# Start of layer 0 in a two-layer trunk kernel: other queues for two loads, splits ahead of norms, 1/rms spread by transposes

## The chip, the cores and the metric

The kernel runs on one core of a Trainium2 chip, as one launch. The metric is the device time of that core in microseconds, as a median over runs. Engines are TensorE (PE; its weight loads are shown as PEld), VectorE (DVE), ScalarE (ACT), GpSimd (POOL) and SyncE (SP), which here only issues transfers.

## What is computed

Two layers of a gated block on 512 tokens of width 1024, all in float32. Cut to what matters:

```python
xn = rmsnorm(x, norm1_g[i])
u_pool, q, k, v, g_a, g_b = split(xn @ w_in[i])          # 1024 -> 6144
q = rotary(rmsnorm(q, q_norm_g[i])); k = rotary(rmsnorm(k, k_norm_g[i]))
lam = exp(sum(lam_q1*lam_k1)) - exp(sum(lam_q2*lam_k2)) + lam_init
a = softmax(q1 @ k1.T * scale) - lam * softmax(q2 @ k2.T * scale)   # chunk-causal
attn = rmsnorm(a @ v, subln_g[i]) * (1 - lam_init)
merged = sigmoid(g_a) * pool_mixer(u_pool) + sigmoid(g_b) * attn
x = x + merged @ w_out[i]
hn = rmsnorm(x, norm2_g[i]); gate, up = split(hn @ w_ffn_in[i])
x = x + (silu(gate) * up) @ w_ffn_out[i]
```

## The kernel before

Every float32 operand of a large product is split in two: a high part, which ScalarE writes by a rounding copy (line 195), and a low part, which VectorE writes as the difference (line 196). A product is then a triple of matmuls: high by high, high by low, low by high (lines 264 to 266, and 473 to 475 in the first block). Weights come in pieces of 512 KB (`piece`, line 209, on SyncE's queue), seven raw buffers and six split ones deep.

In layer 0 the norm of x isn't applied ahead of the products. x comes already transposed (`in_x_t`), is scaled by the gain of the norm, from a small table `scale` of 12 KB (line 410, on ScalarE's queue; read at 458, 460 and 461), and split; 1/rms of each token is put in afterwards. `first_step(i)` loads and splits two of the eight k slices of x and of the first block's weights (q and k of head 3); the first of the four steps goes in halves of 256 KB. Ahead of it TensorE runs `WARM` matmuls on zeros. For the k slices of steps 0 and 1 all four token tiles are multiplied in turn; then, in `attention`, token by token those of steps 2 and 3, with `token_stats` behind the first: it sums the squares over the partitions with a column of `ones` and writes 1/rms to `stats[:, 1, :]` by a power on GpSimd (line 438).

Behind each token's q and k come the squares on ScalarE (600), a power on GpSimd (296), the scaling on VectorE (604) and the rotation (399 to 404). The transposes of the result (`turn`, line 285) are put off: `later(delay, what)` stores a step with a due time on a clock that counts TensorE's columns, and `run_due` runs what is due ahead of each triple of a `product`. So transposes, scores, probabilities and merges lie between the products of the next block. `spread_rms` is such a step: it brings 1/rms into a row that all partitions hold (`rms_row`), as the product of an all-ones matrix with a diagonal one; line 652 multiplies by that row.

The second block is v and the gate of head 3. Its four pieces are asked for by `wblock(KD)` behind the loop over the tokens of the first block, and then SyncE loads the vectors for lambda and the residual x. For all later blocks `wblock` stands ahead of the loop. The order that the program is written in gives the priorities; which instruction an engine's queue holds next is settled ahead of the run by a scheduler that models when each is ready, and an engine then runs its queue in order. `tc.issue_after(ins)` puts the instructions written under it behind `ins` in their engine's queue.

Of the kernel before, what the change touches and what calls it, by code (L numbers as in the profile page):

```python
# [10 lines left out]
F32 = mybir.dt.float32  # L11
# [7 lines left out]
P = 128  # L19
# [15 lines left out]

RAWS, SPLITS = 7, 6

WARM = 11

ROUNDS = ((0, 8), (8, 16), (16, 22))  # L40

# [66 lines left out]
def trunk_kernel(  # L108
# [80 lines left out]
    plan = weight_plan()  # L189
    at = [0]  # L190
    transfers = []

    def split(hi, lo, src):

        ins = nc.scalar.copy(hi, src)  # L195
        nc.vector.tensor_sub(lo, src, hi.bitcast(F32))  # L196
        return ins

    def split_half(hi, lo, src):
# [4 lines left out]
    def piece(raw=None):  # L204
        i = at[0]
        at[0] += 1
        if raw is None:
            raw = sb.tile([P, 2, 512], F32, name="raw", tag="raw", bufs=RAWS)
        transfers.append(nc.sync.dma_start(raw.rearrange("p a b -> p (a b)"), wts[i]))
        hi = sb.tile([P, 2, 512], F32R, name="whi", tag="whi", bufs=SPLITS)  # L210
        lo = sb.tile([P, 2, 512], F32R, name="wlo", tag="wlo", bufs=SPLITS)
        split(hi, lo, raw)
        return [(hi[:, a, :], lo[:, a, :]) for a in range(2)]

    def loaded():
# [190 lines left out]
    def token(t):  # L406
        return slice(t * P, (t + 1) * P)


    nc.scalar.dma_start(scale, scales)  # L410
    cold = sb.tile([P, 512], BF16, name="cold", tag="mt", bufs=3)
    nc.vector.memset(cold, 0.0)
    loaded_table = sb.tile([P, 1], F32, name="table", tag="sso", bufs=4)
# [27 lines left out]
    def first_step(i):  # L441

        xr = sb.tile([P, 2, S], F32, name="xr", tag="raw", bufs=RAWS)
        wr = wraws[i // 2][:, i % 2 * 2:(i % 2 + 1) * 2, :]
        hi = sb.tile([P, 2, 512], F32R, name="whi", tag="whi", bufs=SPLITS)
        lo = sb.tile([P, 2, 512], F32R, name="wlo", tag="wlo", bufs=SPLITS)
        assert at[0] == i
        at[0] += 1
        for ks in ((slice(0, 1), slice(1, 2)) if not i else (slice(0, 2),)):
            nc.sync.dma_start(xr[:, ks, :], x_t[i].rearrange("p (a s) -> p a s", a=2)[:, ks, :])  # L450
            nc.sync.dma_start(wr[:, ks, :], wts[i].rearrange("p (a s) -> p a s", a=2)[:, ks, :])
        for ks in ((slice(0, 1), slice(1, 2)) if not i else (slice(0, 2),)):
            split(hi[:, ks, :], lo[:, ks, :], wr[:, ks, :])
            for a in range(ks.start, ks.stop):
                k = 2 * i + a
                g = scale[:, L * KD + k:L * KD + k + 1]
                if k:
                    nc.scalar.activation(xh[:, k, :], xr[:, a, :], AF.Copy, scale=g)
                else:
                    nc.vector.tensor_scalar_mul(xh[:, k, :], xr[:, a, :], g)  # L460
                nc.vector.scalar_tensor_tensor(xl[:, k, :], xr[:, a, :], g, xh[:, k, :].bitcast(F32), op0=ALU.mult, op1=ALU.subtract)
        sq = sb.tile([P, 2, S], F32, name="sq", tag="mj", bufs=2)
        nc.scalar.activation(sq, xr, AF.Square)
        if i:
            nc.vector.tensor_add(squares[0], squares[0], sq)
        else:
            squares.append(sq)
        return [(2 * i + a, hi[:, a, :], lo[:, a, :]) for a in range(2)]
# [17 lines left out]

    def spread_rms():

        diag = sb.tile([P, S], F32, name="diag", tag="ta", bufs=2)
        for t in range(NT):  # L490
            nc.vector.tensor_scalar_mul(diag[:, token(t)], ident, stats[:, 1, t:t + 1])
        row = mm_ps()
        nc.tensor.matmul(row, lhsT=ones, rhs=diag, start=True, stop=True)
        clock[0] += 4 * S
        nc.scalar.copy(rms_row, row)

    later(2 * QK_WAIT, spread_rms)

    for layer in range(L):
        lam_init = 0.8 - 0.6 * math.exp(-0.3 * layer)  # L500
# [12 lines left out]
        def attention(j, before, then):  # L513
# [9 lines left out]
            def turn(t, qn):  # L523
                tp = tr_ps()
                for h in range(4):
                    transpose(tp[:, h * P:(h + 1) * P], qn[:, h, :])
                split(qh[:, :, token(t)], ql[:, :, token(t)], tp.rearrange("p (h c) -> p h c", h=4))
                later(SCORE_WAIT, lambda: scores(t))

            def scores(t):  # L530
# [51 lines left out]
                ready.add((layer, j, "mj", t))  # L582

            at_start = not layer and j == ORDER[0]
            if not at_start:
                w = wblock(KD)
            for t in range(NT):
                if at_start:
                    acc = first_acc[t]
# [21 lines left out]
                need(*((layer, before, "o", t) for t in range(NT)))  # L611
            vh, vl = pair("v", "v", 2)
            tb = [sb.tile([P, 2, VD], F32, name="tb", tag="tb", bufs=2) for _ in range(2)]
            w = wblock(KD)
            if at_start:
                with tc.issue_after(transfers[-1].ins):
                    for i in range(L):
                        nc.sync.dma_start(lams[i].rearrange("p a b c -> p (a b c)"), spread(rows[i][R_LAM:R_LAM + 4 * QK]))
                    for t in range(NT):
                        nc.sync.dma_start(res[t], x[token(t), :])  # L620
                lambdas()
            for t in range(NT):
                acc = mm_ps()
                product(acc, list(zip(x_tok(t), w)))
# [6 lines left out]
                        v_at(vl, t), acc[:, :VD], rms, v_at(vh, t).bitcast(F32), op0=ALU.mult, op1=ALU.subtract)  # L631
                nc.scalar.activation(tb[t // 2][:, t % 2, :], acc[:, VD:], AF.Tanh, scale=0.5 if layer else stats[:, 2, t:t + 1])
                ready.add((layer, j, "v", t))
            return mj

        def pool_weights(j):
# [323 lines left out]
```

## Time and profile before

| | us |
|---|---|
| median of 3 runs | 1448.56 |
| lowest, highest | 1448.25, 1449.23 |
| the profiled execution | 1447.66 |
| its span, first to last instruction | 1445.8 |
| TensorE busy | 1433.3 |
| VectorE busy | 990.7 |
| ScalarE busy | 689.1 |
| GpSimd busy | 114.3 |

The profile is one execution; its time is the span and about 1.9 us around it. A line of it names the engine, the line of the kernel, the operation, the tile written and those read. A matmul's recorded duration overlaps the next one, so TensorE's pace is read from one start to the next. The idle time before an instruction stands in brackets with what released it.

### The profile page before, as it was taken

Reading aid. Unit: us, or ns where it says so; the run is one execution under the profiler, and the core shown is the slowest. Engines: PE = TensorE matmul, PEld = TensorE weight load, DVE = VectorE, ACT = ScalarE, POOL = GpSimd, SP = SyncE. Lnnn points to the kernel's source line nnn. Section 1 sums busy time; section 2 is a strip of 40 time slices with the busy share of each in tenths; the row PEclk is TensorE's granted clock in tenths of the full one; section 3 lists DMA queues with packets and bytes.
Section 4 is the critical chain, followed back from the end, with each engine's and each line's share of the span. In section 5 each row is a group of like instructions: output and inputs, shape, how many; then the busy total and the mean of one; then the engine's idle time right before and its main releaser. Section 6 shows DMA issues by size and latency. Waiting matters only on the chain.

```text
span 1445.8 us, 21597 instructions
## 1 busy us (share of the span) xinstructions
PE 1433.3 (99%) x8375; PEld 1262.3 (87%) x8375; DVE 990.7 (69%) x1839; ACT 689.1 (48%) x1309; POOL 114.3 (8%) x146
## 2 busy tenths in 40 slices
PE   9999999999999999999999999999999999999999
PEld 6888888888899889989888888888888998999897
DVE  7768677677898548737576685665759975587462
ACT  6544353443666337516354443434546763464350
POOL 1010000000001001001010001001000110010000
PEclk9999999999999999999999999999999999999999
DMA  9311231224258457718322132222422683585361
GB/s 346 110 59 62 94 115 58 88 78 119 59 151 217 115 143 175 208 44 220 130 88 81 59 113 75 83 73 74 123 68 73 178 217 113 128 190 167 73 161 58
DMA packets 50071, 173.02 MB, mean 120 GB/s; under 512 B 5681, under 2 KB 6577, under 8 KB 49969
## 3 DMA queue, kind: packets, MB, share of 16 engines
q1 hardware_dynamic: 39744, 137.02, 28.4%
q0 software_dynamic: 8928, 32.51, 12.6%
q10 hardware_dynamic: 1296, 2.11, 0.6%
q8 instruction: 66, 1.08, 0.3%
q14 instruction: 37, 0.29, 0.1%
HBM read 169.52 MB, written 2.10 MB: 119 GB/s over the span
## 4 chain that ended last, share of the span: by engine, by line
PE 90%; DVE 5%; issue 2%; DMA 2%; POOL 1%; ACT 1%; POOLq 0%; DVEq 0%; ACTq 0%
PE mm L264 19%; PE mm L266 19%; PE mm L265 19%; PE mm L279 5%; PE mm L276 5%; PE mm L278 5%; PE sc L278 2%; PE sc L279 2%; PE sc L276 2%; PE tr L285 2%; PE tr L279 1%; PE tr L276 1%; PE tr L278 1%; DMA wlo<-in_wts 1%; DVE wlo L196 1%
## 5 line engine op out<-in xcount | busy, mean ns | idle before, releaser
L195 ACT CAST whi<-raw 128x1024 fp32r<-128x1024 f32 (+1 forms) x227 | 236.5, 1047 | 211.4 <-issue 119.2
L196 DVE TENSOR_TENSOR wlo<-raw,whi 128x1024 fp32r<-128x1024 f32 (+1 forms) x227 | 274.3, 1215 | 78.2 <-ACT whi L195 75.3
L264 PE MATMUL mm<-whi,xh 128*128 128x512 f32 x480 | 192.2, 400 | 0.0
L265 PE MATMUL mm<-wlo,xh 128*128 128x512 f32 x480 | 187.9, 391 | 0.5 <-DVE wlo L196 0.5
L266 PE MATMUL mm<-whi,xl 128*128 128x512 f32 x480 | 187.6, 391 | 0.0
L703 DVE TENSOR_TENSOR res<-mm,res 128x512 f32<-128x512 f32 (+1 forms) x97 | 66.1, 683 | 118.5 <-PE mm L266 118.5
L266 PE MATMUL mm<-whi,fl 128*128 128x512 f32 (+1 forms) x358 | 138.5, 387 | 0.0
L264 PE MATMUL mm<-whi,fh 128*128 128x512 f32 (+1 forms) x358 | 138.3, 387 | 0.0
L265 PE MATMUL mm<-wlo,fh 128*128 128x512 f32 (+1 forms) x358 | 138.2, 387 | 0.0
L296 POOL TENSOR_TENSOR r<-r,mhalf 128x1 f32<-128x1 f32 (+1 forms) x76 | 57.3, 754 | 649.1 <-DVE r L295 570.0
L266 PEld LDWEIGHTS mm<-whi,xl 128*128 128x128 f32 x480 | 90.1, 188 | 19.7 <-issue 0.2
L265 PEld LDWEIGHTS mm<-wlo,xh 128*128 128x128 f32 x480 | 90.4, 188 | 17.3 <-DVE wlo L196 0.8
L264 PEld LDWEIGHTS mm<-whi,xh 128*128 128x128 f32 x480 | 90.3, 188 | 16.9
L276 PE MATMUL mm<-xqh,whi 128*128 128x256 f32 x352 | 100.4, 285 | 2.7 <-ACT cah L800 2.7
L232 POOL DMA_DIRECT2D wlo<-in_wts x62 | 54.4, 877 | 609.7 <-ACT wlo L231 276.4
L264 PE MATMUL mm<-xh,whi 128*128 128x512 f32 x256 | 102.1, 399 | 0.0
L279 PE MATMUL mm<-xqh,wlo 128*128 128x256 f32 x352 | 100.3, 285 | 1.5 <-DVE wlo L196 1.5
L278 PE MATMUL sc<-xql,whi 128*128 128x256 f32 x352 | 100.0, 284 | 0.8 <-DVE xql L196 0.8
L276 PE MATMUL mm<-xrh,whi 128*128 128x256 f32 x352 | 100.1, 284 | 0.0
L278 PE MATMUL mm<-xql,whi 128*128 128x256 f32 x352 | 100.0, 284 | 0.0
L266 PE MATMUL mm<-xh,wlo 128*128 128x512 f32 x256 | 99.9, 390 | 0.0
L279 PE MATMUL mm<-xrh,wlo 128*128 128x256 f32 x352 | 99.9, 284 | 0.0
(204 smaller groups left out, 3516.5 us busy)
## 6 DMA issues: line engine op xcount, KB each, us to landing
raw<-in_wts SPq DMA_DIRECT2D x243, 512.0 KB, 4.3
wlo<-in_wts POOLq DMA_DIRECT2D x62, 512.0 KB, 7.8
res<-in_x SPq DMA_DIRECT2D x4, 512.0 KB, 8.7
pwr<-in_pool_w ACTq DMA_DIRECT2D x8, 256.0 KB, 2.7
out<-res SPq DMA_DIRECT2D x7, 256.0 KB, 2.0
xr<-in_x_t SPq DMA_DIRECT2D x3, 512.0 KB, 8.0
g<-in_gains SPq DMA_DIRECT2D x6, 256.0 KB, 3.4
xr<-in_x_t SPq DMA_DIRECT2D x2, 256.0 KB, 4.6
```

The source lines that it names most:

```text
L195: ins = nc.scalar.copy(hi, src)
L196: nc.vector.tensor_sub(lo, src, hi.bitcast(F32))
L232: nc.gpsimd.dma_start(lo.rearrange("p a b -> p (a b)"), wts[piece_no], accum_op=ALU.add)
L264: nc.tensor.matmul(acc, lhsT=ah, rhs=bh, start=i == 0, stop=False)
L265: nc.tensor.matmul(acc, lhsT=ah, rhs=bl, start=False, stop=False)
L266: nc.tensor.matmul(acc, lhsT=al, rhs=bh, start=False, stop=i == n - 1)
L276: nc.tensor.matmul(acc[:, i, :], lhsT=ah, rhs=bh, start=start and not i and not k, stop=False, skip_group_check=True)
L278: nc.tensor.matmul(acc[:, i, :], lhsT=ah, rhs=bl, start=False, stop=False, skip_group_check=True)
L279: last = nc.tensor.matmul(acc[:, i, :], lhsT=al, rhs=bh, start=False, stop=i == 1 and k == 3, skip_group_check=True)
L285: nc.tensor.transpose(dst, src, ident)
L296: nc.gpsimd.tensor_tensor(r, r, mhalf[:, :width], op=ALU.pow)
L703: nc.vector.tensor_add(res[t][:, cs], here, res[t][:, cs])
```

## The change

- The table of scales is loaded over GpSimd's queue instead of ScalarE's.
- The first half-piece of weights goes over ScalarE's queue instead of SyncE's; SyncE's other transfers keep their order.
- Ten warm-up matmuls instead of eleven.
- The second block's weights are asked for and split in the program ahead of the loop over the first block's tokens, as in the later blocks. The q/k splits of tokens 1 to 3 are queued behind the last of these splits on their engines.
- `spread_rms` transposes, for each token tile, the column of 1/rms repeated 128 times, into a bank of the transposes' PSUM buffers; no diagonal matrix is made. It is due 81600 columns of the clock after it is stored, instead of 40800, and moves the clock on by 1024 instead of 2048.
- The lambda arithmetic stands behind the second token's values instead of ahead of the first's.

```diff
--- before.py
+++ after.py
@@ -35,7 +35,7 @@
 
 RAWS, SPLITS = 7, 6
 
-WARM = 11
+WARM = 10
 
 ROUNDS = ((0, 8), (8, 16), (16, 22))
 
@@ -189,11 +189,13 @@
     plan = weight_plan()
     at = [0]
     transfers = []
+    last_hi, last_lo = [], []
+    first_v = []
 
     def split(hi, lo, src):
 
         ins = nc.scalar.copy(hi, src)
-        nc.vector.tensor_sub(lo, src, hi.bitcast(F32))
+        last_lo[:] = [nc.vector.tensor_sub(lo, src, hi.bitcast(F32))]
         return ins
 
     def split_half(hi, lo, src):
@@ -209,7 +211,7 @@
         transfers.append(nc.sync.dma_start(raw.rearrange("p a b -> p (a b)"), wts[i]))
         hi = sb.tile([P, 2, 512], F32R, name="whi", tag="whi", bufs=SPLITS)
         lo = sb.tile([P, 2, 512], F32R, name="wlo", tag="wlo", bufs=SPLITS)
-        split(hi, lo, raw)
+        last_hi[:] = [split(hi, lo, raw)]
         return [(hi[:, a, :], lo[:, a, :]) for a in range(2)]
 
     def loaded():
@@ -407,7 +409,7 @@
         return slice(t * P, (t + 1) * P)
 
 
-    nc.scalar.dma_start(scale, scales)
+    nc.gpsimd.dma_start(scale, scales)
     cold = sb.tile([P, 512], BF16, name="cold", tag="mt", bufs=3)
     nc.vector.memset(cold, 0.0)
     loaded_table = sb.tile([P, 1], F32, name="table", tag="sso", bufs=4)
@@ -448,7 +450,7 @@
         at[0] += 1
         for ks in ((slice(0, 1), slice(1, 2)) if not i else (slice(0, 2),)):
             nc.sync.dma_start(xr[:, ks, :], x_t[i].rearrange("p (a s) -> p a s", a=2)[:, ks, :])
-            nc.sync.dma_start(wr[:, ks, :], wts[i].rearrange("p (a s) -> p a s", a=2)[:, ks, :])
+            (nc.sync if i or ks.start else nc.scalar).dma_start(wr[:, ks, :], wts[i].rearrange("p (a s) -> p a s", a=2)[:, ks, :])
         for ks in ((slice(0, 1), slice(1, 2)) if not i else (slice(0, 2),)):
             split(hi[:, ks, :], lo[:, ks, :], wr[:, ks, :])
             for a in range(ks.start, ks.stop):
@@ -486,15 +488,12 @@
 
     def spread_rms():
 
-        diag = sb.tile([P, S], F32, name="diag", tag="ta", bufs=2)
+        row = tr_ps()
         for t in range(NT):
-            nc.vector.tensor_scalar_mul(diag[:, token(t)], ident, stats[:, 1, t:t + 1])
-        row = mm_ps()
-        nc.tensor.matmul(row, lhsT=ones, rhs=diag, start=True, stop=True)
-        clock[0] += 4 * S
+            transpose(row[:, token(t)], stats[:, 1, t:t + 1].broadcast_to([P, P]))
         nc.scalar.copy(rms_row, row)
 
-    later(2 * QK_WAIT, spread_rms)
+    later(4 * QK_WAIT, spread_rms)
 
     for layer in range(L):
         lam_init = 0.8 - 0.6 * math.exp(-0.3 * layer)
@@ -524,7 +523,11 @@
                 tp = tr_ps()
                 for h in range(4):
                     transpose(tp[:, h * P:(h + 1) * P], qn[:, h, :])
-                split(qh[:, :, token(t)], ql[:, :, token(t)], tp.rearrange("p (h c) -> p h c", h=4))
+                with ExitStack() as behind:
+                    if at_start and t:
+                        for ins in first_v:
+                            behind.enter_context(tc.issue_after(ins))
+                    split(qh[:, :, token(t)], ql[:, :, token(t)], tp.rearrange("p (h c) -> p h c", h=4))
                 later(SCORE_WAIT, lambda: scores(t))
 
             def scores(t):
@@ -582,8 +585,9 @@
                 ready.add((layer, j, "mj", t))
 
             at_start = not layer and j == ORDER[0]
-            if not at_start:
-                w = wblock(KD)
+            w = wblock(KD)
+            if at_start:
+                first_v.extend(i.ins for i in last_hi + last_lo)
             for t in range(NT):
                 if at_start:
                     acc = first_acc[t]
@@ -611,14 +615,14 @@
                 need(*((layer, before, "o", t) for t in range(NT)))
             vh, vl = pair("v", "v", 2)
             tb = [sb.tile([P, 2, VD], F32, name="tb", tag="tb", bufs=2) for _ in range(2)]
-            w = wblock(KD)
-            if at_start:
+            if not at_start:
+                w = wblock(KD)
+            else:
                 with tc.issue_after(transfers[-1].ins):
                     for i in range(L):
                         nc.sync.dma_start(lams[i].rearrange("p a b c -> p (a b c)"), spread(rows[i][R_LAM:R_LAM + 4 * QK]))
                     for t in range(NT):
                         nc.sync.dma_start(res[t], x[token(t), :])
-                lambdas()
             for t in range(NT):
                 acc = mm_ps()
                 product(acc, list(zip(x_tok(t), w)))
@@ -631,6 +635,8 @@
                         v_at(vl, t), acc[:, :VD], rms, v_at(vh, t).bitcast(F32), op0=ALU.mult, op1=ALU.subtract)
                 nc.scalar.activation(tb[t // 2][:, t % 2, :], acc[:, VD:], AF.Tanh, scale=0.5 if layer else stats[:, 2, t:t + 1])
                 ready.add((layer, j, "v", t))
+                if at_start and t == 1:
+                    lambdas()
             return mj
 
         def pool_weights(j):
```

## Rows read from the trace of the kernel before

**Rows 1.** Page, part 1: busy us, share of the span, instructions.

```profile
PE 1433.3 (99%) x8375; PEld 1262.3 (87%) x8375; DVE 990.7 (69%) x1839; ACT 689.1 (48%) x1309; POOL 114.3 (8%) x146
```

**Rows 2.** Chain that ended last, 0 to 8 us: start us, us, what.

```profile
0.74 4.24 DMA scale<-in_scales
5.01 0.50 DVE xh L460
...
6.20 0.69 DVE wlo L196
6.94 0.50 PE tr L475
7.44 0.23 PE tr L473
```

**Rows 3.** Timeline, SyncE's queue and ScalarE: start us, us, engine, line, operation.

```profile
0.74 0.39 SPq L450 DMA_DIRECT2D xr<-in_x_t  x1
1.19 0.42 SPq L451 DMA_DIRECT2D raw<-in_wts  x1
...
2.47 0.20 ACT L414 ACTIVATE table<-cold 128x1 f32<-128x1 bf16 x1
```

**Rows 4.** Timeline of ScalarE and TensorE: start, us, [idle before <-releaser].

```profile
5.44 0.62 ACT L195 CAST whi<-raw 128x512 fp32r<-128x512 f32 x1 [2.77 <-DMA raw<-in_wts]
6.87 0.72 ACT L458 ACTIVATE xh<-xr,scale 128x512 fp32r<-128x512 f32 x1 [0.82 <-DMA xr<-in_x_t]
...
1.19 4.88 PE L419 MATMUL mm<-cold 128*128 128x512 bf16 x11 [1.19 <-DVE cold L412]
...
9.84 0.19 PEld L475 LDWEIGHTS tr<-wlo,xh 128*128 128x128 f32 x1 [0.31 <-DVE wlo L196]
```

**Rows 5.** GpSimd's queue: line 232, one issue, its first packets; ScalarE's queue, 1.7 to 2.0.

```profile
DMA to landing us min/median/max: 5.4/7.8/9.1
...
424.64 0.86 POOL L232 DMA_DIRECT2D wlo<-in_wts  x1 [13.46 <-ACT wlo L231]
...
q0 software_dynamic: 15, 0.06, 293.8%
...
q10 hardware_dynamic: 3, 0.00, 0.8%
```

**Rows 6.** TensorE's waits, 0 to 120 us: us in total, times, longest.

```profile
PE tr L285 <- DVE ql L196: 0.8, 1, 0.8
```

**Rows 7.** Timeline of TensorE, 30 to 37 us.

```profile
30.10 0.63 PE L285 MATMUL tr<-ident,qn 128*128 128x128 f32 x4
30.48 0.48 PE L264 MATMUL mm<-whi,xh 128*128 128x512 f32 x1
30.80 0.40 PE L265 MATMUL mm<-wlo,xh 128*128 128x512 f32 x1
...
35.02 0.48 PE L264 MATMUL mm<-whi,xh 128*128 128x512 f32 x1
36.01 0.50 PE L265 MATMUL mm<-wlo,xh 128*128 128x512 f32 x1 [0.50 <-DVE wlo L196]
```

**Rows 8.** VectorE: its waits, 20 to 40 us; timelines of VectorE and ScalarE.

```profile
DVE qn L604 <- POOL r L296: 1.5, 2, 0.9
DVE stats L439 <- POOL stats L438: 0.8, 1, 0.8
...
34.72 1.23 DVE L196 TENSOR_TENSOR wlo<-raw,whi 128x1024 fp32r<-128x1024 f32 x1
...
25.63 2.01 ACT L195 CAST whi<-raw 128x1024 fp32r<-128x1024 f32 x2
```

**Rows 9.** The chain at 40 to 43 us; the first reader of the row.

```profile
40.20 0.44 PE tr L285 x4
...
41.57 1.03 PE mm L493 x2
...
L652 DVE TENSOR_TENSOR up<-mm,rr x8: 680/684/692, 123.8 to 338.7; 128x512 f32<-128x512 f32 x8
```

## The prediction

> **What bounds the kernel now.** I read the page's busy table first: TensorE is busy 99% of the span [rows 1], so a change pays only where TensorE stands still, or where TensorE itself is given less to do. What is left to gain in the part that the change touches, the first 100 us of layer 0, is then read from three views. The chain of waits for the first 7 us shows what TensorE waits for before its first products: not the weights but the small table of scales, 4.24 us on its way, then two VectorE steps [rows 2]. The list of TensorE's waits shows the only two long stalls of the first 100 us that a releaser is named for: 0.5 us for a low part of a weight piece (line 196), and 0.8 us for a low part of q/k, later [rows 6, 7]. And the timeline of TensorE round 30 to 42 us shows where these lie, and one dear matmul pair, the spreading of 1/rms [rows 7, 9]. All times below are of the profiled execution, 1447.66 us (span 1445.8); the three timed runs have their median 0.9 us above it, so my sum is made on 1447.66 and 0.9 is added at the end.
>
> **Part 1, the start (scales to GpSimd's queue, first weight half-piece to ScalarE's, one warm-up matmul less).** Now SyncE issues the first x half at 0.74 and the first weight half at 1.19; ScalarE's queue issues the scales at 0.74 [rows 2, 3]. The weight half now goes out at 0.74 from ScalarE, and each later transfer on SyncE moves up one slot, 0.45 us (1.19 less 0.74). The weight half landed just before ScalarE's cast at 5.44 [rows 4]; it can land up to 0.45 earlier, and no more. The row beside it is the Trainium skill's "Trainium Kernel Development and Optimization", section Key Constraints: transfers issued from SP, ACT and POOL run on the same 16 engines and interleave, so a second issuing queue saves only issue time. By that rule this edit alone is worth 0.45 us at most, which is the end that the rows give; no row here has two queues with large transfers side by side at the start.
>
> But the cast was not last: the chain goes scales landed (4.98), scaled x at 5.01 on VectorE, low x, low weights at 6.20, third product at 6.94 [rows 2]. So the scales decide, and they move to the software queue. For that queue the trace has 62 transfers, all later and all of 512 KB: landing 5.4 to 9.1 us after issue [rows 5]. In a quiet moment, one issued at 424.64 has its first 15 packets between 426.1 and 426.4, at least 1.46 us after issue; on ScalarE's queue the first three packets of the scales came by 2.0 and none before 1.7, about 1.0 us after issue [rows 5]. So I take 0.5 us later for the scales, which are 12 KB: landing near 5.5 instead of 4.98. From there VectorE needs the same 1.93 us to the third product (6.94 less 5.01), so it starts at 7.45, 0.5 later. (The Trainium skill's "DMA: Bandwidth & Descriptors", section Specifications, gives about 1 us to the first byte on the GpSimd path and 0.6 on the others, a difference of 0.4; the trace, 1.46 against 1.0, agrees. By the page the start would be 0.1 us better than I have it.) Behind it TensorE's weight loads wait for a split of the second k slice, 0.31 before 9.84 [rows 4]. A late start eats this wait as long as ScalarE's own chain, which starts with the second x half at 6.87 and needs no scales before that [rows 4], doesn't move; about 0.3 us is given back. Sum: +0.2 us. Bounds: -0.45 (scales no later, everything up one slot) and +0.9 (scales as slow as the fastest software transfer, 5.4 after issue, so landed at 6.14: +1.16 less 0.3).
>
> The eleven warm-up matmuls take 4.88 us from 1.19 [rows 4], 0.44 each by division, and end at 6.07, when the first product follows at 6.11. They wait for nothing else and nothing waits for them but this. With ten they end near 5.6: no gain while data come at 6.1, and half a microsecond of TensorE idle. I cost it at nothing; the cover is the data wait. If TensorE lost its full rate over that pause, each of the twelve products of the first k step would take as long as a warm-up matmul, 0.44 instead of the 0.23 that one costs in the chain [rows 2]: 12 times 0.21, +2.5 us. That is a rival below.
>
> **Part 2, the second block's splits ahead of the norms.** Now the low part of the fourth piece is made at 34.72 to 35.95, between the norms of the third and fourth tokens [rows 8], and TensorE, which has begun that k step at 35.02, starts its second product only at 36.01; after a turn the same pair is 0.32 apart (30.48 to 30.80) [rows 7]. So 0.99 less 0.32, 0.67 us, is stall, and it goes, since ScalarE casts the last two pieces at 25.63 already [rows 8], so they lie in memory by then. What it costs: two splits of 1.2 us on VectorE stand ahead of the first tokens' norms, 2.4 us, and two casts on ScalarE. The first norm's result must be at TensorE at 30.10, where its four transposes stand ahead of the second block's products [rows 7]. VectorE is idle 1.5 and 0.8 us in exactly that stretch, 20 to 30 us, waiting for GpSimd's powers [rows 8]: 2.3 of the 2.4 us fit into idle time. I take no added wait at 30.10; bounds 0 to +2.3. New waits: the q/k splits of tokens 1 to 3 wait for the last split of the second block. Behind them in ScalarE's and VectorE's queues stand the value products' own evictions, but those splits are then long done. Sum: -0.7, bounds -0.7 and +1.6.
>
> **Part 3, 1/rms by transposes.** The fp32 product over 512 columns held TensorE 1.03 us; four transposes of one tile take 0.44 [rows 9]. So -0.6 us of work on the bound engine. No row has a transpose whose source is one column repeated; between the two ends (0.44 and, if the repeated read is as slow as the old product, 1.03) I take 0.44, because the source has the same 128x128 size as in the transposes shown. Bounds -0.6 and 0. More than 0.6 can't be won, as four transposes remain. VectorE loses four products with the identity, which lie beside other work: nothing. The step also moves from 40800 to 81600 columns of the clock, some 18 us later (40800 columns at 0.23 us for 512), from 41.57 to near 59 us. What it feeds is first read at 123.8 [rows 9], so its one eviction on ScalarE can wait for idle time: nothing.
>
> **Part 4, the rest.** The lambda work goes behind the second token's values; its result is first read by the epilogue of the scores, which are later still: nothing. The written order after 40 us shifts by less than one triple of products (the clock is moved on by 1024 columns instead of 2048). That can remove the wait of 0.8 us near 78 us [rows 6] or make another like it: 0, bounds -0.8 to +0.8.
>
> **Sum.** 0.2 - 0.7 - 0.6 + 0 = -1.1 us: 1446.56 on the profiled execution, 1447.5 against the median of 1448.56.
>
> **The rivals.**
> One, on the other side: the software queue is slow, and the kernel is slower. Place: VectorE's first instruction at 5.01, which waits for the scales, and everything behind it on TensorE. The gains elsewhere are 1.3 us and 0.3 is absorbed, so it decides from a landing 1.6 us later than now, 5.8 us after issue. For it: the median of that queue is 7.8 us [rows 5]; that would be +3.6 - 0.3 - 1.3 = +2.0, 1450.6. Against: those carry 512 KB, this one 12.
> Two: the first weight half doesn't come earlier. In the program's order it stands behind the activation that loads ScalarE's table, which ended at 2.67 [rows 3]. Issued there, it lands 4.2 us later at 6.9, its cast and low part end 1.3 us later, third product at 8.2: +1.25 - 0.3 - 1.3 = -0.35, 1448.2. For it the order; against it, the present order of engines departs from the program's freely (a product stands inside another's triple at 41.57 [rows 9]), and the transfer waits for nothing.
> Three: a wait takes the place of the one removed: norms late at 30.10 by the full 2.3 us, which gives -1.1 + 2.3 = +1.2, 1449.8. For it: both engines run in order. Against: the idle of VectorE.
> Four: TensorE's rate falls in the longer pause: -1.1 + 2.5, 1450.0.
>
> **How the numbers follow.** Forecast 0.62, rival one 0.1, two 0.12, three 0.1, four 0.06. Forecast's own range by its bounds, which won't all fall on one side: 1446.0 to 1449. To leave out no more than two in ten the range reaches into rivals two and three, and half a microsecond below the bounds, since the three timed runs alone lie 1.0 us apart: 1445.4 to 1449.8. About 0.2%, 2.9 us, is what a measurement of this kernel can tell from no change; only all bounds together pass it on the fast side (-0.45 - 0.7 - 0.6 - 0.8 = -2.55, and a lower draw of the median): 0.07. On the slow side two rivals would have to meet: 0.06. So same 0.87.
>
> **What would show it.** Start: VectorE's first scaled x moves from 5.01 to about 5.5, third product from 6.94 to about 7.4; earlier than 6.94 breaks part 1, later than 8 means rival one or two (the issue row of the weight half on ScalarE tells which). Part 2: no wait for line 196 near 35 us, and none over 0.5 us at the first transposes. Part 3: four transposes of about 0.1 us each from the statistics near 59 us and no fp32 product. Were TensorE's idle in the first 100 us more than 1 us different from this account, the prediction is wrong in its reasons even if the time holds.

## The result, and the profile after

Timed beside each other, 22 runs each, the changed kernel has a median of 1449.41 us (1447.53 to 1452.22) and the kernel before 1446.42 (1445.69 to 1449.23): ratio 1.0018, 95% interval 1.0012 to 1.0025. The change costs about 3 us. The predicted 1447.5 was a gain of 1.1 on the 1448.56 of the three first runs, which lie high among the runs of that kernel (the other 19 have a median of 1446.24). So the time fell inside the range, and the direction was wrong. That it fell inside is luck: set on 1446.42, the forecast range would have ended at 1447.7.

One row of the changed kernel answers to [rows 1] and says little (page, part 1):

```profile
PE 1431.9 (99%) x8376; PEld 1262.4 (87%) x8376; DVE 989.2 (68%) x1835; ACT 688.2 (48%) x1309; POOL 114.6 (8%) x147
```

TensorE is busy 1.4 us less than before, and yet this execution (1449.24, span 1447.4) is 1.6 us longer than the one profiled before. So the time lies where TensorE waits, or in its clock.

The start answers to [rows 2] to [rows 4]: timelines of the changed kernel (start us, us, engine, line, operation, idle before and its releaser).

```profile
0.74 0.41 ACTq L453 DMA_DIRECT2D raw<-in_wts  x1
1.28 0.70 POOL L412 DMA_DIRECT2D scale<-in_scales  x1 [0.83 <-POOLq L959]
5.15 0.62 ACT L197 CAST whi<-raw 128x512 fp32r<-128x512 f32 x1 [2.47 <-DMA raw<-in_wts]
6.19 0.49 DVE L462 TENSOR_SCALAR xh<-xr,scale 128x512 fp32r<-128x512 f32 x1 [4.87 <-DMA scale<-in_scales]
1.19 4.42 PE L421 MATMUL mm<-cold 128*128 128x512 bf16 x10 [1.19 <-DVE cold L414]
6.83 0.47 PE L475 MATMUL tr<-whi,xh 128*128 128x512 f32 x1 [1.22 <-DVE xh L462]
...
8.13 0.50 PE L477 MATMUL tr<-wlo,xh 128*128 128x512 f32 x1
```

The weight half goes out early and ScalarE's cast starts 0.29 us earlier than in [rows 4]. But GpSimd issues the scales at 1.28, not at 0.74, and they free VectorE only at 6.19, against 5.01 in [rows 2]. Everything behind moves with it: the third product from 6.94 to 8.13, and TensorE stands still 1.22 us behind its warm-ups.

What follows that pause is in the next view: TensorE in windows of 1 us (window, its length, busy us and matmuls, granted clock, DMA share, GB/s).

```profile
8.00:9.00 1.00, 0.89 (x5) 0.93 1.04 426
9.00:10.00 1.00, 1.00 (x4) 0.50 1.02 418
10.00:11.00 1.00, 1.00 (x4) 0.50 1.02 418
11.00:12.00 1.00, 1.00 (x4) 0.50 1.02 418
12.00:13.00 1.00, 1.00 (x5) 0.86 1.02 418
```

From 8.9 to 12.3 the granted clock is 0.50, the 1.2 GHz level, and products that take 0.23 us each at 1.00 start 0.43 apart: by the windows 3.4 us at half rate, 1.7 us lost. The profile of before has 1.00 in all these windows.

At the second block, in place of [rows 7], the timeline of TensorE in the changed kernel shows:

```profile
32.13 0.39 PE L266 MATMUL mm<-whi,xh 128*128 128x512 f32 x1
33.85 0.63 PE L287 MATMUL tr<-ident,qn 128*128 128x128 f32 x4 [1.33 <-DVE qn L406]
```

And that of VectorE, in place of [rows 8]:

```profile
26.92 0.17 DVE L441 TENSOR_SCALAR stats<-stats 128x4 f32<-128x4 f32 x1 [0.79 <-POOL stats L440]
27.14 1.22 DVE L198 TENSOR_TENSOR wlo<-raw,whi 128x1024 fp32r<-128x1024 f32 x1
...
29.63 0.35 DVE L608 SCALAR_TENSOR_TENSOR qn<-tr,r,hg 128x128 f32<-128x128 f32 x1 [1.00 <-POOL r L298]
29.90 1.22 DVE L198 TENSOR_TENSOR wlo<-raw,whi 128x1024 fp32r<-128x1024 f32 x1
31.03 0.86 DVE L608 SCALAR_TENSOR_TENSOR qn<-tr,r,hg 128x128 f32<-128x128 f32 x3
...
32.14 0.38 DVE L405 TENSOR_TENSOR m<-qn,tab 128x64 f32<-128x64 f32 x2
33.15 0.35 DVE L608 SCALAR_TENSOR_TENSOR qn<-tr,r,hg 128x128 f32<-128x128 f32 x1 [0.63 <-POOL r L298]
33.42 0.28 DVE L406 TENSOR_TENSOR qn<-m,m 128x128 f32<-128x128 f32 x1
```

The same steps of VectorE in the kernel before:

```profile
25.35 0.17 DVE L439 TENSOR_SCALAR stats<-stats 128x4 f32<-128x4 f32 x1 [0.79 <-POOL stats L438]
...
29.40 0.35 DVE L604 SCALAR_TENSOR_TENSOR qn<-tr,r,hg 128x128 f32<-128x128 f32 x1 [0.64 <-POOL r L296]
29.67 0.28 DVE L404 TENSOR_TENSOR qn<-m,m 128x128 f32<-128x128 f32 x1
```

The wait for line 196 is gone, and a new one of 1.33 us stands at the first transposes. The rows of VectorE say why. Two splits of 1.22 us stand inside the norm chain: one at 27.14, right behind the statistics (26.92), and one at 29.90, between the scaling of the first token's first head (29.63) and of its other three (31.03). From the statistics to the last step of the first token's rotation (line 406, at 33.42) it takes 6.5 us; in the kernel before, from 25.35 to 29.67, it took 4.3. VectorE's idle time was no cover: its waits for GpSimd in the chain are as long as before (0.79, 1.00 and 0.63 us, against 0.79, 0.91 and 0.64), and the splits, which stand between its links in an in-order queue, came on top of them. The last step of the rotation is queued behind the scaling of the second token, which itself waits 0.63 us for GpSimd; that was so before as well (29.40).

The row of 1/rms, in place of the 1.03 us of [rows 9] (timeline of TensorE):

```profile
59.81 0.60 PE L287 MATMUL tr<-ident,stats 128*128 128x128 f32 x4
60.24 0.27 PE L287 MATMUL tr<-ident,pr 128*128 128x128 f32 x1
```

0.43 us from start to start. The marker for all of it is the first reader of that row, which [rows 9] has at 123.8 (its line of the groups: count, ns min/median/max, first and last start):

```profile
L658 DVE TENSOR_TENSOR up<-mm,rr x8: 680/683/692, 125.9 to 340.6; 128x512 f32<-128x512 f32 x8
```

The changed kernel is 2.1 us behind there. A marker is that of one execution: warm8 below, which is the kernel before with three warm-ups fewer, starts its first product 0.9 us earlier (5.25) and has the marker at 122.8.

### The profile page after: what moved, and what is told of

Its sections match the earlier page's. It is cut to its first block, busy times and chain, and to the rows that moved or that the text cites. A ratio compares the mean times of both kernels' runs of the same rounds, so it can differ in the third digit from the quotient of the medians.

```text
span 1447.4 us, 21599 instructions
## 1 busy us (share of the span) xinstructions
PE 1431.9 (99%) x8376; PEld 1262.4 (87%) x8376; DVE 989.2 (68%) x1835; ACT 688.2 (48%) x1309; POOL 114.6 (8%) x147
## 3 DMA queue, kind: packets, MB, share of 16 engines
q8 instruction: 66, 1.08, 0.3%
## 4 chain that ended last, share of the span: by engine, by line
PE 90%; DVE 5%; issue 2%; DMA 2%; POOL 1%; ACT 1%; POOLq 0%; DVEq 0%; ACTq 0%
PE mm L266 19%; PE mm L268 19%; PE mm L267 19%; PE mm L281 5%; PE mm L278 5%; PE mm L280 5%; PE sc L280 2%; PE sc L281 2%; PE sc L278 2%; PE tr L287 2%; PE tr L281 1%; PE tr L280 1%; PE tr L278 1%; DMA wlo<-in_wts 1%; DVE wlo L198 1%
## 5 line engine op out<-in xcount | busy, mean ns | idle before, releaser
L278 PE MATMUL sc<-xqh,whi 128*128 128x256 f32 x352 | 99.9, 284 | 0.0
L267 PE MATMUL mm<-xl,whi 128*128 128x512 f32 x256 | 99.8, 390 | 0.0
```

The costliest lines, as they stand in the source:

```text
L267: nc.tensor.matmul(acc, lhsT=ah, rhs=bl, start=False, stop=False)
L278: nc.tensor.matmul(acc[:, i, :], lhsT=ah, rhs=bh, start=start and not i and not k, stop=False, skip_group_check=True)
```

## The experiments

The theory after this profile: three losses, (a) late scales, (b) a fall of the clock behind the pause they make, (c) the wait in VectorE's order at the first transposes. The rivals: the later weight or row steps cost more than they show, or one of the three hides the others. Each kernel below has 11 runs beside 27 to 33 of the kernel before on the same chip. "Below 1.0" counts those of the 11 runs whose mean granted clock over the span is 0.999 or less; the kernel before has 64 such among 152 in these comparisons.

| kernel | median less before's, us | ratio, 95% | below 1.0 |
|---|---|---|---|
| start_only | +1.33 | 1.0001 to 1.0018 | 11 |
| scale_only | +1.90 | 0.9998 to 1.0016 | 8 |
| weight_act | -0.35 | 0.9986 to 1.0004 | 5 |
| undo_scale | +0.70 | 0.9993 to 1.0011 | 6 |
| bridge | +0.25 | 0.9990 to 1.0008 | 4 |
| warm8 | +0.92 | 0.9992 to 1.0010 | 7 |
| splits_only | +1.26 | 1.0001 to 1.0019 | 3 |
| row_only | +0.12 | 0.9992 to 1.0010 | 7 |
| no_start | -0.32 | 0.9989 to 1.0007 | 3 |
| later_turn | -1.99 | 0.9975 to 0.9993 | 2 |
| full_bridge | -0.61 | 0.9985 to 1.0002 | 5 |
| best | -0.72 | 0.9980 to 0.9998 | 6 |
| full_later | -0.39 | 0.9985 to 1.0003 | 4 |
| full_bridge_later | -0.47 | 0.9985 to 1.0003 | 8 |
| later_warm13 | -1.05 | 0.9983 to 1.0001 | 6 |
| change_side | +2.35 | 1.0005 to 1.0023 | 11 |
| full_later_side | -1.06 | 0.9983 to 1.0001 | 4 |
| start_only_side | +1.08 | 1.0000 to 1.0018 | 10 |

### The start: which load, and what does the pause do?

**start_only**: part 1 of the change on the kernel before.

```diff
-WARM = 11
+WARM = 10
...
-    nc.scalar.dma_start(scale, scales)
+    nc.gpsimd.dma_start(scale, scales)
...
-            nc.sync.dma_start(wr[:, ks, :], wts[i].rearrange("p (a s) -> p a s", a=2)[:, ks, :])
+            (nc.sync if i or ks.start else nc.scalar).dma_start(wr[:, ks, :], wts[i].rearrange("p (a s) -> p a s", a=2)[:, ks, :])
```

> The kernel before with part 1 alone: scales over GpSimd's queue, first weight half over ScalarE's, ten warm-up matmuls; splits, norms and the row of 1/rms as before. Theory A (the start is the cause: the scales land late, and the longer pause of TensorE lets its clock fall): third product near 8.1 us instead of 6.94, a stretch at half clock (granted clock 0.50) behind it in most executions, median +2 to +3 us. Theory B (the start costs only the 1.2 us of the late scales, and the half-clock stretch is chance, found as often in the kernel before): +0.7 to +1.2 us. Theory C (the cause is the wait at the first transposes): under +0.5 us.

**scale_only**: of these, only the scales move; eleven warm-ups.

```diff
-    nc.scalar.dma_start(scale, scales)
+    nc.gpsimd.dma_start(scale, scales)
```

> The kernel before with one edit: the scales go over GpSimd's queue; first weight half on SyncE, eleven warm-up matmuls. Theory S (the scales' queue alone makes the late start): scales land 0.6 to 1.3 us later than in the kernel before, first product at 6.4 to 7.0, half-clock stretch behind it unless the one warm-up matmul more bridges it, +1.0 to +1.5 us. Rival W (the weight half over ScalarE's queue crowds out the small transfer, or the missing warm-up matmul makes the stretch): scales near 5.2, 0 to +0.4 us.

**weight_act**: only the weight half moves, queued behind the scales on ScalarE; eleven warm-ups.

```diff
-            nc.sync.dma_start(wr[:, ks, :], wts[i].rearrange("p (a s) -> p a s", a=2)[:, ks, :])
+            (nc.sync if i or ks.start else nc.scalar).dma_start(wr[:, ks, :], wts[i].rearrange("p (a s) -> p a s", a=2)[:, ks, :])
```

> The kernel before with one edit: the first weight half goes over ScalarE's queue, behind the scales there, so SyncE's other transfers move up one slot; scales stay on ScalarE, eleven warm-up matmuls. Theory S: 0, between -0.4 and +0.2 us, as the scales still decide the first product and one issue slot is all there is to win. Rival W: scales land later, +0.5 us or more.

start_only and scale_only show the same start: first scaled x at 5.83 and 5.80, third product at 7.76 and 7.73, and half clock behind it. TensorE's windows of start_only:

```profile
9.00:10.00 1.00, 1.00 (x4) 0.50 1.07 438
10.00:11.00 1.00, 1.00 (x4) 0.50 0.99 406
11.00:12.00 1.00, 1.00 (x4) 0.50 1.06 434
```

So moving the scales alone makes the start late, and the clock falls behind it; one warm-up more did not prevent that. weight_act leaves the scales early, has its third product at 7.04 and a cast only 0.08 earlier than the kernel before, and is not told from it by its time. No form of part 1 showed a gain.

**undo_scale**: the whole change, but the scales back on ScalarE's queue, ahead of the weight half.

```diff
-    nc.gpsimd.dma_start(scale, scales)
+    nc.scalar.dma_start(scale, scales)
```

> The whole change with one edit undone: the scales go over ScalarE's queue again, ahead of the first weight half there; ten warm-up matmuls stay. Theory (the scales over GpSimd's queue make the late start, and the pause that it opens makes the half-clock stretch): first product back near 6.0, no stretch at granted clock 0.50 in the first 14 us or a rare one, -0.2 to -1.0 us against the kernel before, 3 us faster than the change. Rival (it takes the sum of several edits): still +1 us or more.

The scales land 3.6 us after issue and the third product is back at 6.88, but now the first product waits 1.1 us for ScalarE's cast, since the weight half is issued second there, at 1.18. No half clock follows that pause in its profile. At +0.70 it is about 2 us better than the change and no better than before: the wait of 1.3 us at the first transposes is still in it.

**bridge**: start_only with 13 warm-ups, so that the pause is filled and the scales stay late.

```diff
-WARM = 10
+WARM = 13
```

> Part 1 alone, but with thirteen warm-up matmuls instead of ten, so that TensorE has no pause before a first product at 6.5 to 6.8 us. Theory P (the pause lets the clock fall): no stretch at granted clock 0.50 in the first 14 us, and 0.9 to 1.6 us faster than part 1 alone, so -0.3 to +0.4 us against the kernel before. Rival: the stretch comes from somewhere else (the early products with their own gaps): it stays, and the median stays at +1.0 to +1.5 us.

**warm8**: the kernel before with 8 warm-ups, a pause without late scales.

```diff
-WARM = 11
+WARM = 8
```

> The kernel before with eight warm-up matmuls instead of eleven and nothing else: the scales come as before, but TensorE pauses from about 4.8 to the first product near 5.7 to 6.1, about as long as in the change. Theory P (the pause lets the clock fall): a stretch at granted clock 0.50 in the first 14 us in most executions, +0.8 to +1.6 us. Rival (the stretch needs the late first products themselves, not the pause): no stretch, within 0.3 us of the kernel before.

bridge, the timeline of TensorE:

```profile
6.53 0.47 PE L473 MATMUL tr<-whi,xh 128*128 128x512 f32 x1 [0.30 <-DVE xh L460]
```

and its window in which start_only has 0.50:

```profile
9.00:10.00 1.00, 1.00 (x7) 1.00 1.04 426
```

The start is as late as in start_only (third product 7.83), the pause is 0.30, the clock stays at 1.00 there, and the loss is gone: +0.25 instead of +1.33 and +1.90, with 4 of 11 runs below 1.0 instead of 21 of the 22 of start_only. Its first reader of the row is at 123.8, as in the kernel before. So by these profiles a start that is 0.9 us late costs next to nothing there (the stall at line 196 and the second slice's take it up), and what start_only loses is the fall of the clock. warm8 leaves a pause of only 0.47 in its profile and no half clock there; +0.92 with an interval across 1 settles nothing.

### The norms: is it VectorE's order?

**splits_only**: part 2 alone. **no_start**: parts 2 and 3. Of part 2 the core, the rest as in the change:

```diff
+            w = wblock(KD)
+            if at_start:
+                first_v.extend(i.ins for i in last_hi + last_lo)
             for t in range(NT):
...
-                lambdas()
...
+                if at_start and t == 1:
+                    lambdas()
```

> The kernel before with part 2 alone: second block's weights split ahead of the first tokens' norms, q/k splits of tokens 1 to 3 queued behind, lambda later. Theories A and B: the wait of 0.67 us round 35 us goes, a wait of 1 to 1.5 us at the first transposes comes, +0.3 to +0.8 us. Theory C (this is the main loss): +1.5 us or more. My recorded forecast: -0.7 us.

> The changed kernel with part 1 undone: scales on ScalarE's queue, first weight half on SyncE's, eleven warm-up matmuls; parts 2 and 3 as in the change. Theory A: -0.3 to +0.2 us against the kernel before, third product back at 6.94, no half-clock stretch in the first 20 us. Theory B: the same for the place, but half-clock stretches at the start as often as in the change. Theory C: +0.8 us or more, since the wait at the first transposes is still there.

TensorE's waits in the first 130 us of splits_only (what waits, for whom: us, times, longest):

```profile
PE tr L287 <- DVE qn L406: 1.6, 1, 1.6
...
PE mm L495 <- DVE diag L493: 0.8, 1, 0.8
PE tr L287 <- DVE ql L198: 0.7, 1, 0.7
```

The wait at the first transposes comes with part 2, without a late start. A second one is new: the fp32 product of the row now waits 0.8 us for its diagonal, which the late VectorE makes. With the row by transposes (no_start) that is gone and 1.3 is left of the first; the two medians differ by 1.6 us. So by these waits part 3 is worth more behind part 2 than alone; the intervals of the times are too wide to show it.

**later_turn**: no_start, with the first token's transposes four triples later.

```diff
-                later(15000 + 6500 * t if at_start else QK_WAIT, lambda t=t, qn=qn: turn(t, qn))
+                later(max(23500, 15000 + 6500 * t) if at_start else QK_WAIT, lambda t=t, qn=qn: turn(t, qn))
```

> Parts 2 and 3 without part 1, and the first token's transposes put off until four triples of the second block are done (due after 23500 columns instead of 15000). Theory T (the splits ahead cost just the wait at the first transposes, and it is a matter of place): wait of 1.3 us there goes, -1.3 to -1.8 us against the kernel before. Rival: the wait comes back at the next transposes or at the scores, since VectorE is as late as before: -0.3 us, as without the delay.

Its first transposes, in the timeline of TensorE, and its marker, in the groups:

```profile
31.68 0.60 PE L287 MATMUL tr<-ident,qn 128*128 128x128 f32 x4
```

```profile
L658 DVE TENSOR_TENSOR up<-mm,rr x8: 681/684/693, 121.2 to 335.9; 128x512 f32<-128x512 f32 x8
```

No wait, and 121.2 instead of 123.8: 2.6 us ahead of the kernel before. Not all of that is the edits': the first product starts 0.39 earlier in this execution, at 5.72. Against no_start, which differs by this one edit, the wait of 1.3 is gone and the medians, by their distances from the kernel before, are 1.7 apart. At 1444.74 (1443.78 to 1446.32) it is the fastest of all the kernels, 2.0 us under the one before and, by the distances of each from it, 4.3 to 5.0 under the changed one.

**full_bridge**: the whole change with 13 warm-ups.

```diff
-WARM = 10
+WARM = 13
```

> The whole change, but with thirteen warm-up matmuls instead of ten, which reach over the wait for the scales. Theory: the scales are as late as in the change, but the half-clock stretch goes: 1 to 1.6 us faster than the change, +0.8 to +1.8 us against the kernel before. Rival (the stretch isn't tied to the pause): no difference to the change, +2.5 to +3 us.

It came out at -0.61, 3.0 to 3.6 us under the change (+2.35 and +2.99 against the kernel before), which is too much for a pause. The timelines of VectorE, then TensorE, show a second thing that changed with it:

```profile
24.42 0.17 DVE L441 TENSOR_SCALAR stats<-stats 128x4 f32<-128x4 f32 x1 [0.79 <-POOL stats L440]
...
30.03 0.28 DVE L406 TENSOR_TENSOR qn<-m,m 128x128 f32<-128x128 f32 x1
30.23 0.22 DVE L297 TENSOR_SCALAR r<-ss,stats 128x2 f32<-128x2 f32 x1
31.24 0.35 DVE L608 SCALAR_TENSOR_TENSOR qn<-tr,r,hg 128x128 f32<-128x128 f32 x1 [0.79 <-POOL r L298]
```

```profile
30.46 0.63 PE L287 MATMUL tr<-ident,qn 128*128 128x128 f32 x4
```

The scheduler, given three more matmuls, put the last rotation step ahead of the second token's scaling, and the wait of 1.3 us was gone with the same splits ahead of the norms. From the statistics (24.42) to that step it takes 5.6 us, against 6.5 in the change, so 0.9 us of the wait is order in the queue; the statistics also come 0.7 earlier than in change_side below (25.11). It is no test of the pause: the 13 warm-ups ended so early that a pause of 0.99 was there all the same, without a fall.

### The row

**row_only**: part 3 alone.

```diff
-        nc.tensor.matmul(row, lhsT=ones, rhs=diag, start=True, stop=True)
...
+            transpose(row[:, token(t)], stats[:, 1, t:t + 1].broadcast_to([P, P]))
```

> The kernel before with part 3 alone: 1/rms spread by four transposes instead of an fp32 product. All theories: four transposes take 0.43 us on TensorE instead of 1.03; -0.6 us, within -0.2 and -1.0. If it is 0 or slower, the shift of the written order behind it costs what the transposes save.

+0.12 with an interval of 1.3 us to either side: the 0.6 us that its profile shows can't be told from nothing by the time. Measured is the instruction, not the gain.

### What does the whole change pay for each?

**full_later**: the whole change with the later turn. **full_bridge_later**: with 13 warm-ups besides. **later_warm13**: later_turn with 13 warm-ups. **best**: later_turn with the weight half on ScalarE's queue behind the scales. The edits are those above: the due time in the first two on the changed kernel, `WARM = 13` in the second and third, the weight line of weight_act in the fourth.

> The whole change with its ten warm-up matmuls, and only the first token's four transposes due four triples later. Theory (late scales, a pause with its fall of the clock, and a wait of 1.3 us at the first transposes, three separate losses): that wait goes, the half clock at 9 to 12 us stays, so about 1.3 to 2 us better than the whole change, which stood 3.0 above the kernel before: +1.0 to +1.7. Rival (the pause alone makes the change slower, the wait is taken up elsewhere): +2.4 to +3.0.

> The whole change with 13 warm-up matmuls and the later transposes. Theory: the pause is bridged, so no half clock in the first 20 us, and no wait at the first transposes; the late scales stay. The whole change with 13 warm-ups alone, in which that wait was gone as well, stood 0.6 under the kernel before, so this one should stand there too: -0.3 to -1.2. Rival (what 13 warm-ups saved beyond the pause had nothing to do with the wait): the later turn brings its 2 us once more, -2 to -3.

> Splits ahead, row by transposes, later transposes, both loads on their old queues, and 13 warm-up matmuls instead of 11. The first product waits for the warm-ups, some 0.9 us later than now (2 of 0.43 to 0.44 us), of which 0.3 is absorbed at the second k slice. If the clock early in the span plays no part in that kernel (2 of 11 runs below 1.0), it is 0.3 to 0.9 worse than with 11: -1.1 to -1.7. If the fuller start guards the clock: -2.0 or better.

> Weight half on ScalarE's queue behind the scales, which stay there, eleven warm-up matmuls, splits ahead and transposed row as in the change, first token's transposes after four triples of the second block. Expected from the parts: -2.0 (the later turn) and -0.35 (the weight half): -1.8 to -2.6 us against the kernel before. If the weight half gains nothing here: -2.0.

full_later is a miss: it keeps late scales and a pause (0.95 us), and is 3.4 us under the change, not 1.3 to 2. full_bridge_later is no better than full_later, so no gain of a bridge shows once the wait is gone; later_warm13 is 0.9 above later_turn, about as expected of two more warm-ups, though their intervals overlap. best is a miss too: it stood 1.3 above later_turn; in its profile the weight half lands late and the first product waits 1.2 us for the cast. So the sum of three separate losses doesn't hold as it stood, and the next three were timed side by side on one chip.

**change_side**: the change itself. **full_later_side** and **start_only_side**: the two kernels above, again. No new edits.

> The whole change itself, beside the other two. Theory (the fall of the clock behind the pause and the wait at the first transposes are two losses, and the change meets both in most executions): +2.4 to +3.2, with most executions below the clock of 1.0 over the span. Rival (the fall belongs to the chip or session in which the change was timed first): fewer than half below 1.0, and +0.6 to +1.6.

> The whole change with the first token's transposes four triples later, again, now beside the change itself. If its 0.4 under the kernel before came of the wait alone, it is 1.3 to 1.7 under the change here. If the later turn also keeps the clock up, it is 3 or more under the change, while the change has most executions below 1.0 and this one less than half. If the chip or session made the difference, both have the same share of executions below 1.0.

> Only the start (scales over GpSimd's queue, first weight half over ScalarE's, ten warm-ups), again, beside the change. It had all of 11 executions below 1.0 and +1.3. If the fall at the start belongs to these kernels, most executions are below 1.0 again, +0.9 to +1.7; if to the chip or session, fewer than half, and about 0.

The change is +2.35, full_later -1.06, 3.4 us apart once more; all 11 runs of the change are below a clock of 1.0, 4 of full_later's. The chip is not the reason. The profiled execution of change_side is the useful one: late scales (5.98), a pause of 0.97, and no fall behind it. TensorE's windows, its first transposes and the marker:

```profile
0.00:20.00 20.00, 17.50 (x65) 1.00 0.90 332
380.00:390.00 10.00, 10.00 (x87) 1.00 0.57 129
390.00:400.00 10.00, 8.42 (x63) 0.93 0.32 107
400.00:410.00 10.00, 10.00 (x78) 0.90 0.63 165
```

```profile
32.03 0.63 PE L287 MATMUL tr<-ident,qn 128*128 128x128 f32 x4 [1.32 <-DVE qn L406]
```

```profile
L658 DVE TENSOR_TENSOR up<-mm,rr x8: 678/682/691, 124.1 to 338.9; 128x512 f32<-128x512 f32 x8
```

Same kernel, marker at 124.1 here and at 125.9 in the execution with half clock; third product 7.91 and 8.13. Less that 0.2, the fall cost 1.6 us. Without it the change is 0.3 behind the profile of the kernel before at the marker. And its clock falls at another place, round 400 us, where the profile of the kernel before has its own fall.

The account of change_side, then. The mean clocks of its 11 runs lack 1.36 thousandths on average, those of the kernel before 0.52. In the kernel before, the runs at 0.999 have a mean of 1447.99 and those at 1.0 of 1446.26: 1.7 us for a thousandth. That makes 1.4 us for the clock, by estimate, and 0.3 by the marker: 1.7 of the 1.9 by which the means differ.

Two things on record make that 0.3 uncertain. It hangs on one profile of the kernel before, whose first scaled x (5.01) is the latest of the ten profiled kernels with the scales on ScalarE's queue (4.01 to 4.61 in the other nine); against warm8's marker of 122.8 it would be 1.3. And at an equal mean clock of 0.999 the 7 such runs of change_side have a mean of 1448.55 and the 11 of the kernel before beside it 1447.99, so 0.6 is left without the clock. Two runs of the change in its first comparison show a clock of 1.0 and still took 1449.11 and 1450.08, 2.7 and 3.7 us above the median of the kernel before beside them; this account doesn't explain them.

The same sum for the later turn: for full_later_side against change_side it is 1.7 by the marker (122.4) and 1.0 thousandth, together 3.4, where the means differ by 2.9.

## Why the prediction was wrong

**Direction: it was wrong, in part 1 and part 2.** What bounds the kernel, the two stalls and the dear matmul pair were read right. The sum was -1.1; without a fall of the clock the steps came to +0.3 by the profiles (0.6 at an equal clock), and the clock adds most of the rest, by estimate.

**"So I take 0.5 us later for the scales": mis-sized.** They came 1.18 later (0.97 in change_side). The sum counted the way from issue to landing and took both issues for 0.74. GpSimd's first issue starts at 1.28 and takes 0.70 us: 0.54 of the delay lies there, and no row of before shows GpSimd's first issue. The landing is 4.9 us after issue (4.7 in change_side), against 4.24 in [rows 2]. The difference of 0.4 that the Trainium skill's "DMA: Bandwidth & Descriptors" gives (section Specifications) is near that part alone; the measurement, 1.0 to 1.2 in all, decides. Even that is against the slowest landing: over the ten profiled kernels with either queue the first scaled x starts at 5.9 (GpSimd's) and 4.3 (ScalarE's) in the median, 1.6 apart. The upper bound, from the fastest transfer of [rows 5], put the landing at 6.14, and that is where it fell, at 6.2: the end was right, but by luck: it took 0.74 and 5.4 us, where 1.28 and 4.9 were measured. "0.3 is absorbed" was too low: of 0.97, 0.44 was left at the end of the first block (last product from 29.65 to 30.09).

**"I cost it at nothing; the cover is the data wait": failed.** The sign was lost without it (+0.3), but by the account above the clock makes most of the size. The cover went with the late scales, which the same part forecast: the pause grew from none to about 1 us. Rival four had the mechanism and its price (2.5 against 1.6 measured) but a chance of 0.06. In how many of the change's runs the fall comes at this place isn't known: of its two profiled executions one has it there, the other round 400 us. Half clock right behind the start is in 4 of 10 profiled executions with a pause of 0.86 us or more there, and in none of 10 with 0.5 or less. All four have late scales; in undo_scale and best, whose scales are early and whose pause of 1.1 to 1.2 us ends with the cast, there is none. That the place of such a fall changes from run to run agrees with the Trainium skill's "TensorE: Matmul & The Clock Gate" (section What's actually happening): the chip's watch on the engine isn't reset when a kernel starts.

**"2.3 of the 2.4 us fit into idle time. I take no added wait": failed.** The stall of 0.67 near 35 us went, as predicted, and 1.3 came at the first transposes: rival three at just over half its price. None of the splits fitted: the chain from the statistics to the last step of the rotation grew by 2.2 us, from 4.3 to 6.5, and 1.3 of that reached TensorE. I added up idle time in a stretch and did not ask between which instructions of the chain it lay.

**Part 3 held**: 0.43 for 1.03, near 59 us. **Part 4 held**: the wait of 0.8 near 78 us [rows 6] and one of 0.3 behind it became one of 0.9. **Rival two** did not happen: the weight half is issued at 0.74.

The working closes on change_side: 0.44 for the start, 1.3 for the wait at the first transposes, -0.67 for the stall that went, -0.6 for the row and -0.2 for the later waits make +0.3, and so says the marker. Beside the terms, the chances were wrong: rivals one, three and four were priced one at a time, and all three came, each below its price. The late scales of the first make the pause of the fourth, so they were never separate cases.

**Open.** Why the clock falls in so many runs of the change: 31 of its 33 are below 1.0, and 21 of 22 of start_only, but 8 of 22 of full_later, which has the same start and nearly as long a pause. Late scales with a pause and a fall were shown in start_only, scale_only and the change, and their repair by bridge; that the later turn repairs it too is seen and not explained. Nor are the two slow runs of the change at a clock of 1.0. Only one execution of each kernel is profiled, so where the clock falls in the others isn't known. I did not try another order of the norm chain with the change's own due times.

## What to carry to other kernels

Idle time of an in-order engine covers moved work only if it lies where that work can be queued without standing between two links of a chain; read the order round the idle time, not its sum. Filler that keeps TensorE busy is costed against the arrival that ends it: where a change makes that arrival later, it needs more filler, not less. When two edits touch one chain, price their bad cases together; and here the cheapest repair was the due time of the consumer, with which the same splits and the transposed row came out 2 us under the kernel before.

## What the runs showed of the hardware

- GpSimd's first transfer is issued at 1.28 us and takes 0.70 to issue; the first ones of SyncE and ScalarE start at 0.74 and take about 0.4. The 12 KB land 4.4 to 4.9 us after issue there, and 3.2 to 4.2 on ScalarE's queue, in ten profiled kernels each.
- A pause of TensorE of about 1 us behind ten to thirteen warm-ups was followed, 1.6 to 2.1 us later, by 3.4 us at a granted clock of 0.50, in 4 profiled executions and not in 6 others.
- The warm-ups' length varies from run to run: ten took 3.85 to 4.45 us, thirteen 4.43 to 5.73. Three more of them are no sure bridge. The granted clock reads 1.00 there, although most warm-ups start 0.43 us apart, as the products of the same 512 columns do at 0.50; so it doesn't tell their rate.
- A fall can come late as well: round 390 to 410 us in 6 of 20 profiled executions, after TensorE had stood still for 1.6 us there, as it does in all 20; and near 1110 us in two.
